# Dilated attention: a maximum pass over 66 rows and value products of 128 columns

## The chip, the cores and the metric

One core of one Trainium2 chip runs the whole program. The metric is the device time of one execution in microseconds (us), as the median of several runs. The engines are TensorE (PE, matrix products, with a queue of its own for loading weights, PEld), VectorE (DVE), ScalarE (ACT), GpSimd (POOL) and SyncE (SP, which issues transfers). The granted TensorE clock is given as a share of 2.4 GHz: 1.00 is that level and 0.50 is 1.2 GHz.

## What is computed

Two transformer blocks over 1024 tokens. The change lies in the second block, in its attention of eight heads of 64 channels: three dilated causal patterns, each with its own softmax, joined by their log sums. That is the same as one softmax in which a pair of tokens counts as often as patterns hold it.

```python
DILATED_PATTERNS = ((128, 1), (512, 4), (2048, 16))

def _dilated_attention(q, k, v):
    ...
    for window, dil in DILATED_PATTERNS:
        ...
        o, lse = _banded_causal_attention(by_stride(q), by_stride(k), by_stride(v), window // dil)
        ...
    wts = jax.nn.softmax(jnp.stack(lses), axis=0)
    o = jnp.sum(wts[..., None] * jnp.stack(outs), axis=0)
    return o.transpose(0, 2, 1, 3)

def second_block(...):
    ...
        o = _dilated_attention(q, k, v)
        o = _rmsnorm(o, attn_norm_gain[l].reshape(ATTN_HEADS, HEAD_DIM)).astype(x.dtype)
        y_attn = o.reshape(B, S, ATTN_WIDTH)
        x = x + jnp.concatenate([y_rwkv, y_attn], axis=-1) @ w_out[l]
```

## The kernel before

Large products are made of pairs of rounded float32 pieces (fp32r, high and low part); in the trace such a product is one matmul record. Products of plain float32 are two records each, one after the other, each with its own weight load.

The attention (`attn`) works head by head, and each head in 12 pieces: a piece is one block of 128 keys (k) against up to 512 queries (half ch of the tokens). For each piece:

- `score` makes the scores by keys in two products: L1811 over 128 rows (the high part of q and its remainder, stacked in `qq`, against the high part of k twice in `kk`) and L1812 over 66 rows (64 rows of the remainder of k in `kl` against the high part of q in `qm`, and two rows in which `kl` is one and `qm` holds minus the maximum of each query, as high and low part).
- `masked` adds the mask on DVE (tile pT, L149), and ACT takes the exponential (L159).
- `gather` multiplies blocks of 128 queries of pT with the values (L1834). The values of a pair of heads lie in `vx` as [128 tokens, 8 blocks, 2 heads, 65]: 64 channels and a one, so that the 65th column of the product is the sum of the weights. Plain float32: 36 products a head, 72 records. The sums stand in bank "a" as [128, 4, 65].

The maximum of a query is found ahead, for a later head, in `attn_max`: 12 pairs of products a head, L1728 over 128 rows and L1729 over 64 rows, after each pair a reduction on DVE (L1730); then a transposition (L1736), two small operations (mh) and two transfers over DRAM that bring the maxima into rows 64 and 65 of `qm`. `attn_heads` makes the operands of a head: four loads, copies of q and k on ACT (L1706, L1709, L1712), two subtractions of about 2.4 us on POOL (qq, kl). `qm` and `kl` have three buffers, taken in turn.

The order on PE, DVE and ACT is written out by hand: score of piece p+1, mask of p, one or two steps of `attn_max` or `attn_heads` of a later head (`ahead`), exponential of p, gather of p-1, a step of transpositions (`attn_values` L1757, `attn_norm` L1789) and, from the second head on, a step of `mix_rwkv` (L1582, the output projection of the other half of the block). POOL and SP, and the group norm of the recurrence that still runs beside the first two heads (L1554, tiles yn, bon, gn, yr), are placed by a scheduler. The maxima of head 0 are found before the loop, beside the end of the recurrence.

Lines below are those of the kernel before; the changed kernel's lie one or two further on.

Of the kernel before, what the change touches and what calls it, by code (L numbers as in the profile page):

```python
# [8 lines left out]
F32 = mybir.dt.float32  # L9
# [3 lines left out]
ALU = mybir.AluOpType  # L13
# [4 lines left out]
P = 128  # L18
# [14 lines left out]
NT = 256            # tokens of a stretch around the recurrence  # L33
NU = T2 // P        # its stretches, of four chunks each
SLOT = 1056
FILL = 12           # piece of the attention from which on the recurrence goes through the output projection
NMM = 3             # accumulator banks of the large products

CH1 = [(0, 352), (352, 696), (696, 1040)]
F0 = 12             # first token that the channel mixer of block 1 sees  # L40
HF = 514            # half of its tokens
# [7 lines left out]
class Build:  # L49
    def __init__(self, ctx, tc, I, out):  # L50
        self.tc, self.nc, self.I, self.out = tc, tc.nc, I, out
        self.const = ctx.enter_context(tc.tile_pool(name="const", bufs=1))
        self.glob = ctx.enter_context(tc.tile_pool(name="glob", bufs=1))
        self.tags = {"XHa": (self.glob, 4), "XHb": (self.glob, 4), "XLa": (self.glob, 4), "XLb": (self.glob, 4), "R": (self.glob, 1), "T": (self.glob, 3)}
        self.wp = ctx.enter_context(tc.tile_pool(name="wp", bufs=2))
        for t in ("wraw", "whi", "wlo"):
            self.tags[t] = (self.wp, 2)
        self.dr = ctx.enter_context(tc.tile_pool(name="dr", bufs=1, space=DRAM))
        self.n, self.sm, self.nsq, self.rdg = 0, None, 2, "T"
        self.turn = {"XH": 1, "XL": 1}      # tags whose slots lie in two sets, taken in turn  # L60

# [6 lines left out]
    def region(self, name, **tags):  # L68
        """a stretch of the program with its own working memory: slots by tag, and small tiles."""
# [9 lines left out]
    def then(self, outer, first, tags, second):  # L79
        """the Y slots through, over them the first region's tags and, from the call of what it yields, the mixer's."""  # L80
# [10 lines left out]
    def psum(self, ctx):  # L91
        """the eight banks of the accumulators: three for the large products, the others by use."""
        self.pp = ctx.enter_context(self.tc.tile_pool(name="ps", bufs=1, space=PSUM))
        self.use, self.nq, self.nmm = {}, 0, 0
        self.big = [f"m{i}" for i in range(NMM)]      # those of the large products
# [14 lines left out]
    def pack(self, sizes, name="pk", tag="S"):  # L110
        """one slot cut into [128, n] pieces."""
# [32 lines left out]
    def store(self, out, in_):  # L144
        """a transfer that waits for data just made: not in the way of the loads."""
# [15 lines left out]
    def split(self, src, shape, name="hl", hi_eng="act", tag=("XH", "XL")):  # L161
        """src (float32) as the exact sum of two float32r tiles."""
# [12 lines left out]
    def weights(self, segs, gain=None):  # L175
        """segs of (source [kt*128 rows, m columns], k offset, column offset) as one [128, kt, m] (hi, lo) pair,
        rows scaled by gain [128, kt]."""
# [15 lines left out]
    def mm3(self, ps, a, b, start, stop, **kw):  # L193
        """ps += a^T b for a, b given as (hi, lo) float32r pairs."""
# [5 lines left out]
    def proj(self, w, rhs, chunks, sink, m0=0, m=P):  # L200
        """sink(ci, a, b, psum[m, b-a]) for each chunk of w^T rhs; w (hi, lo) [128, kt, *]."""
# [9 lines left out]
    def constants(self):  # L211
# [7 lines left out]
        self.triu = self.cst([P, P], name="triu")         # 1 where row <= column  # L219
# [3 lines left out]
        self.sgn = self.cst([P, 1], name="sgn")           # 1 on the upper partitions, -1 on the lower ones  # L223
# [7 lines left out]
    def more_constants(self):  # L231
        nc = self.nc
        self.mpos = self.cst([P, P], name="mpos")         # 0 where row <= column, else huge
# [13 lines left out]
    def params(self, specs):  # L247
        """Vectors of length n*128 as columns: {name: AP [128, n]}."""
# [39 lines left out]
    def add_sums(self, ps, src, start, stop):  # L288
        """ps [128, blocks] += the sums over partitions of src, tokens on the partitions."""
# [8 lines left out]
    def rstd(self, ps, w, n, out=None):  # L298
        """(ps / n + eps)^-0.5 for w tokens, on every partition: an accumulator, or out."""
# [15 lines left out]
    def square_acc(self, acc, src, j, a, b, scale=1.0):  # L315
        """acc[:, a:b] gathers the squares of the tiles j = 0, 1, .."""
# [7 lines left out]
    def square_sum(self, ps, src, start, stop, scale=1.0):  # L324
        """ps += the sums over partitions of the squares of src."""
# [5 lines left out]
    def rstd_chunk(self, out, acc, a, b, n):  # L331
        """out[:, a:b] = (sum over partitions of acc[:, a:b] / n + eps)^-0.5 on every partition."""
# [37 lines left out]
    def spill_x(self):  # L370
        """the residual stream to DRAM while the mixer runs."""
# [24 lines left out]
    def reduce_angle(self, r, x, shape):  # L396
        """r = x mod 2 pi in [-pi, pi]."""
# [6 lines left out]
    def angle_tables(self, cos, sin, rhi, rlo, idx, ng, n, work, sgn):  # L404
        """cos and sin (times a sign per partition) of idx * r for idx [128, n], r = rhi + rlo [128, ng]."""
# [18 lines left out]
    def ssm_params(self):  # L424
# [43 lines left out]
        self.tt(ais, ais, mg, ALU.mult)          # [im; -im] of abar^j  # L468
        nsg = self.cst([P, 1], name="nsg")
        self.ts(nsg, self.sgn, -1.0, ALU.mult)  # L470
        self.ts(ain, ais, nsg[:, 0:1], ALU.mult)         # -im on both halves
        self.ts(ars, ar, self.sgn[:, 0:1], ALU.mult)     # [re; -re]
        self.ars, self.ain = ars, ain
        # input matrices, discretised: z = (abar - 1) / lambda
# [14 lines left out]
        self.ts(zi, zi, nsg[:, 0:1], ALU.mult)   # [-im; im]  # L489
# [15 lines left out]
        # abar^(7-r)  # L505
# [5 lines left out]
        # output matrices  # L511
# [11 lines left out]
        self.c1s, self.dd = (g16(t) for t in self.pack([512, 512], "c1s", "Y"))     # [re; -im]  # L523
        self.dd = self.dd[:16]
        self.ts(self.c1s, self.c1, self.sgn[:, 0:1], ALU.mult)
        # feed-through on the diagonal
# [6 lines left out]
    def ssm_tables(self, j):  # L533
        """lhsT matrices of the eight groups of batch j: chunk input to state, within chunk, state to output."""
# [43 lines left out]
    def ssm_in(self, j):  # L578
        """projection of channels 128 j.. of u, regrouped as [(step, channel), group, chunk]."""
# [54 lines left out]
    def ssm_out(self, j, dy):  # L634
        """gelu of the branch, channels on partitions, tokens in order."""
# [24 lines left out]
    def qko(self):  # L660
        """q and k after convolution and silu, tanh(o / 2), by heads, to DRAM."""
# [15 lines left out]
    def values(self):  # L677
        """v by tokens (with a column of ones) and the input and forget gates by tokens."""
# [36 lines left out]
    def gate_math(self):  # L715
# [11 lines left out]
        # log sigmoid: min(f, 0) - log(1 + exp(-|f|))  # L727
# [19 lines left out]
        # running maximum within each chunk  # L747
# [6 lines left out]
        # running maximum over chunks, on one partition  # L754
# [37 lines left out]
    def conv_qk(self, j, j0, dst):  # L792
        """causal convolution of four taps and silu of tile j of [q, k]."""
# [15 lines left out]
    def mlstm_head(self, h):  # L809
# [57 lines left out]
        # h = num / max(|den|, exp(-m)); then the rms over the head  # L867
# [43 lines left out]
    def merge_a(self, ya):  # L911
        """four times the state space branch, gated."""
# [9 lines left out]
    def merge_b(self, ma, yb):  # L922
        """four times the gated sum of the branches, split."""
# [17 lines left out]
    def rows(self, weights, rhs, ch, acc, sink, scale, apart, between={}):  # L941
        """all output tiles for the token chunks ch, and the inverse rms of what sink returns of them, by chunks;
        apart: the last two tiles chunk by chunk. between[j]: what comes in after tile j."""
# [28 lines left out]
    def mix_out(self, mg, leave):  # L972
        """x += rmsnorm(merged w_out); normed, the operands of the channel mixer."""
# [58 lines left out]
    # The first products go by halves of the channels (the even and the odd tiles of x), of the hidden tiles and of the tokens, seven products of  # L1032
    # halves for eight: with a = w^T = [[a11, a12], [a21, a22]], x = [[x11, x12], [x21, x22]] and
    #   s1 = a21 + a22, s2 = s1 - a11, s3 = a11 - a21, s4 = a12 - s2,
    #   t1 = x12 - x11, t2 = x22 - t1, t3 = x22 - x12, t4 = x21 - t2:
    #   c11 = a11 x11 + a12 x21,               c12 = a11 x11 + s2 t2 + s1 t1 + s4 x22,
    #   c21 = a11 x11 + s2 t2 + s3 t3 + a22 t4, c22 = a11 x11 + s2 t2 + s3 t3 + s1 t1.
    def unit(self, fx, src, c0, dst, fine=False):
        """dst[i] [128, 2 n] = the products for columns c0 + 128 i .. of src, i = 0, 1."""
# [66 lines left out]
    def hidden(self, fx, w_gate, w_up, cw, cb, func):  # L1106
        """func(conv(x w_gate)) * (x w_up), tile by tile to DRAM."""
# [3 lines left out]
        off = 2 * n - T2                # tokens before the first one of the result  # L1111
        z = max(0, 2 - off)             # zeros before those
# [20 lines left out]
    def down(self, hid, w_down, y, last, each=None, after=None, between=None):  # L1133
        """y tiles [128, 1024] = hid w_down, two hidden tiles at a time; each and after by the last ones' chunks."""
# [32 lines left out]
    def ffn1(self, fx):  # L1167
# [8 lines left out]
        def each(j, a, b):  # L1176
            """the sums of squares: while the second half's products run, and after them."""
# [46 lines left out]
    def constants2(self):  # L1224
        nc, g = self.nc, self.nc.gpsimd
        self.blk = self.cst([P, P], name="blk")          # 1 within a head of 64 channels
# [3 lines left out]
        # masks of the products within a chunk: of removal key and key, tokens of the first on the partitions; of removal and  # L1230
        # receptance; of removal and removal key, where twice the removal comes in
# [9 lines left out]
    def lora_weights(self):  # L1241
        """the up-projections of the low rank maps, split: [hi; hi; lo] for the narrow ones."""
# [891 lines left out]
```

## Time and profile before

| | |
|---|---|
| time, median of 3 runs | 3405.7 us (3387.16, 3406.9, 3405.7) |
| profiled execution, span from first to last instruction | 3405.0 us |
| PE busy | 3186.8 us (94%) |
| DVE, ACT, POOL busy | 2026.2, 1145.8, 1336.8 us |
| mean granted TensorE clock over the span | 0.900 |
| attention loop, from head 0 to the end of head 7 | 2253.0 to 2581.8 us of the span |

The span of the profiled execution is its own time as far as the profile tells; it stands 0.7 us under the median. Busy time of PE is made of records whose ends are modelled, so the distance from the start of one record to the start of the next says more of a product's cost than its length. A row of the timeline gives the start, the length of what is merged in it (x8 is eight records), the engine, the line and the tiles.

### The profile page before, as it was taken

The page shows a single profiled execution, that of the slowest core. Times are in us where ns is not written, and L with a number is a line of the kernel's source. Part 1 is how long each engine was busy: PE and PEld are TensorE (multiplying, and loading weights), DVE is VectorE, ACT ScalarE, POOL GpSimd, SP SyncE. Part 2 cuts the span into 40 slices and gives each one's busy share as a digit, 9 for nine tenths or more (in the row PEclk, how much of TensorE's full clock was granted, in tenths as well). Part 3 has the DMA queues.
Part 4 walks back from the last instruction along what each step waited for, and adds up shares of the span by engine and source line. Part 5 has one row for each costly group of instructions (what it writes and reads, how often), then busy time and mean ns, then how long its engine had stood idle before and what let it go on. Part 6 is the DMA issues. An engine that isn't in the chain of part 4 may idle for free.

```text
span 3405.0 us, 52731 instructions
## 1 busy us (share of the span) xinstructions
PE 3186.8 (94%) x20636; PEld 2789.2 (82%) x20636; DVE 2026.2 (60%) x3567; ACT 1145.8 (34%) x2178; POOL 1336.8 (39%) x1303
## 2 busy tenths in 40 slices
PE   4989999989799999999999898999998799999998
PEld 3989999879799999877777787867767688887777
DVE  4565563674676666466866544464444866665666
ACT  2334323344343344312432333322323433334211
POOL 5666210133554443323531645421101655554431
PEclk7999999989799999999799888855758799999999
DMA  4434422334222222421334544322215222224321
GB/s 134 98 88 109 133 94 60 101 112 134 69 75 75 76 80 92 145 92 52 112 117 151 143 110 116 102 81 68 81 54 181 73 87 75 82 89 157 130 75 56
DMA packets 322534, 336.82 MB, mean 99 GB/s; under 512 B 60081, under 2 KB 270734, under 8 KB 322286
## 3 DMA queue, kind: packets, MB, share of 16 engines
q1 hardware_dynamic: 289646, 310.38, 29.9%
q10 hardware_dynamic: 32640, 23.08, 2.1%
q8 instruction: 162, 2.65, 0.3%
q14 instruction: 86, 0.70, 0.1%
HBM read 232.66 MB, written 96.40 MB: 97 GB/s over the span
## 4 chain that ended last, share of the span: by engine, by line
PE 72%; DVE 9%; issue 4%; POOL 3%; DMA 3%; ACT 3%; SPq 1%; ACTq 0%; DVEq 0%; POOLq 0%
PE pm L196 13%; PE pm L197 13%; PE pm L198 13%; PE px L197 5%; PE px L196 5%; PE px L198 5%; PE pa L1834 3%; PE pm L1729 2%; DVE dn L149 2%; PE pc L1582 1%; PE pc L1502 1%; PE pm L1728 1%; DVE t L149 1%; PE px L292 1%; POOL fs L149 1%
## 5 line engine op out<-in xcount | busy, mean ns | idle before, releaser
L196 PE MATMUL pm<-xh,whi 128*128 128x512 f32 (+5 forms) x1344 | 454.0, 338 | 15.2 <-DVE th L149 9.4
L198 PE MATMUL pm<-xh,wlo 128*128 128x512 f32 (+5 forms) x1344 | 453.0, 337 | 0.9 <-DVE wlo L149 0.9
L197 PE MATMUL pm<-xl,whi 128*128 128x512 f32 (+5 forms) x1344 | 453.2, 337 | 0.0
L149 DVE TENSOR_TENSOR y<-y,pm 128x512 f32<-128x512 f32 (+1 forms) x336 | 218.1, 660 | 159.5 <-PE pm L198 159.1
L196 PEld LDWEIGHTS pm<-xh,whi 128*128 128x128 f32 (+1 forms) x1344 | 263.2, 196 | 38.2 <-DVE th L149 9.8
L196 PE MATMUL pm<-dn,dn 128*128 128x512 f32 (+1 forms) x736 | 285.8, 389 | 6.7 <-DVE y L149 6.3
L197 PE MATMUL pm<-dn,dn 128*128 128x512 f32 (+1 forms) x736 | 282.9, 384 | 0.7 <-POOL dn L149 0.7
L198 PE MATMUL pm<-dn,dn 128*128 128x512 f32 (+1 forms) x736 | 282.6, 384 | 0.0
L198 PEld LDWEIGHTS pm<-xh,wlo 128*128 128x128 f32 (+1 forms) x1344 | 262.6, 195 | 22.2 <-DVE wlo L149 1.3
L197 PEld LDWEIGHTS pm<-xl,whi 128*128 128x128 f32 (+1 forms) x1344 | 263.2, 196 | 20.7 <-issue 0.9
L149 POOL TENSOR_TENSOR dn<-hid,dn 128x1024 fp32r<-128x1024 f32 x44 | 131.8, 3014 | 250.6 <-ACT dn L1141 250.6
L197 PE MATMUL px<-t,sh 128*128 128x258 f32 (+2 forms) x684 | 218.5, 320 | 3.2 <-DVE t L149 3.2
L196 PE MATMUL px<-t,sh 128*128 128x258 f32 (+2 forms) x684 | 216.4, 317 | 1.5 <-DVE up L149 1.5
L198 PE MATMUL px<-t,sl 128*128 128x258 f32 (+2 forms) x684 | 216.2, 316 | 0.0
L149 DVE TENSOR_TENSOR wlo<-wraw,whi 128x1024 fp32r<-128x1024 f32 (+2 forms) x114 | 152.5, 1340 | 82.5 <-ACT whi L170 79.9
L196 PEld LDWEIGHTS pm<-dn,dn 128*128 128x128 f32 x736 | 138.2, 188 | 44.3 <-DVE y L149 14.4
L170 ACT CAST whi<-wraw 128x1024 fp32r<-128x1024 f32 (+2 forms) x114 | 103.2, 906 | 186.4 <-PE pm L197 147.6
L198 PEld LDWEIGHTS pm<-dn,dn 128*128 128x128 f32 x736 | 138.3, 188 | 29.8
L197 PEld LDWEIGHTS pm<-dn,dn 128*128 128x128 f32 x736 | 138.4, 188 | 29.5 <-POOL dn L149 1.2
L149 POOL TENSOR_TENSOR wraw<-wraw,par 128x1024 f32<-128x1024 f32 (+1 forms) x36 | 72.4, 2010 | 191.9 <-DMA wraw<-in_w_in_dram 183.5
L170 ACT CAST dn<-wd 128x1024 fp32r<-128x1024 f32 x44 | 46.1, 1047 | 291.1 <-PE pm L197 290.6
L197 PEld LDWEIGHTS px<-t,sh 128*128 128x128 f32 x684 | 130.5, 191 | 14.4 <-DVE t L149 5.3
(601 smaller groups left out, 9016.0 us busy)
## 6 DMA issues: line engine op xcount, KB each, us to landing
wraw<-in_w_in_dram SPq DMA_DIRECT2D x61, 512.0 KB
dhid<-up SPq DMA_DIRECT2D x44, 512.0 KB
wd<-in_w_ffn_down_dram SPq DMA_DIRECT2D x44, 512.0 KB
hid<-dhid SPq DMA_DIRECT2D x44, 512.0 KB
wra<-in_w_ffn_up_dram SPq DMA_DIRECT2D x33, 512.0 KB
wrb<-in_w_ffn_up_dram SPq DMA_DIRECT2D x33, 512.0 KB
dg<-th SPq DMA_DIRECT2D x16, 514.0 KB
wraw<-in_w_out_dram SPq DMA_DIRECT2D x16, 512.0 KB
```

Of the source, the lines that this page charges most:

```text
L149: (eng or self.nc.vector).tensor_tensor(out=o, in0=a, in1=b, op=op)
L170: self.nc.scalar.copy(hi, src)
L196: nc.tensor.matmul(ps, a[0], b[0], start=start, stop=False, **kw)
L197: nc.tensor.matmul(ps, a[0], b[1], start=False, stop=False, **kw)
L198: nc.tensor.matmul(ps, a[1], b[0], start=False, stop=stop, **kw)
L292: self.nc.tensor.matmul(ps[:bw, i:i + 1], src[:, i * bw:i * bw + bw], self.ones[:, 0:1], start=start and i == 0, stop=stop and i == n - 1)
L1502: nc.tensor.matmul(ps[:, h], maps[c][:, h], S[:, h], start=True, stop=True)
L1582: nc.tensor.matmul(ps, w[:, k], (yh, yl, yh)[q][:, a:b], start=i == 0, stop=i == 11)
L1728: nc.tensor.matmul(ps, qq[:, qs], kk[:, a:bb], start=True, stop=False)
L1729: nc.tensor.matmul(ps, qm[:64, qs], kl[:64, a:bb], start=False, stop=True)
L1834: nc.tensor.matmul(self.po[:, i - 4 * ch], pT[:, i * P - a:i * P - a + P], self.vx[j % 2][:, k, e], start=k == 0 and i == 4 * ch, stop=k = ...
```

## The change

The second product of the maximum pass takes 66 rows of both operands instead of 64. So that the two added rows give nothing, rows 64 and 65 of `qm` are set to zero on POOL when the operands of the head are made; the maxima are written over them later, as before. The value product takes 128 neighbouring columns of the 130 that a pair of heads has in `vx`, from column 0 for the first head and from column 2 for the second, into a bank of [128, 4, 128]; the 64 channels and the sum are picked from columns 0 to 64, or 63 to 127, and the other columns are not used. The rest of the full difference takes out comments and moves no instruction.

```diff
@@ attn_heads
         nc.scalar.copy(qm[:64], raws[0][:64])
+        pool.memset(qm[64:66].bitcast(F32), 0.0)
         yield
@@ attn_max
                 nc.tensor.matmul(ps, qq[:, qs], kk[:, a:bb], start=True, stop=False)
-                nc.tensor.matmul(ps, qm[:64, qs], kl[:64, a:bb], start=False, stop=True)
+                nc.tensor.matmul(ps, qm[:66, qs], kl[:66, a:bb], start=False, stop=True)
@@ gather
             if k == 0:
-                self.po = self.bank([P, 4, 65], "a")
+                self.po = self.bank([P, 4, P], "a")
...
-                nc.tensor.matmul(self.po[:, i - 4 * ch], pT[:, i * P - a:i * P - a + P], self.vx[j % 2][:, k, e],
+                nc.tensor.matmul(self.po[:, i - 4 * ch], pT[:, i * P - a:i * P - a + P],
+                                 self.vx[j % 2][:, k].rearrange("p e v -> p (e v)")[:, 2 * e:2 * e + P],
                                  start=k == 0 and i == 4 * ch, stop=k == last)
...
-                    nc.scalar.copy(on[:, bs, e], po[:, :, :64])
-                    nc.scalar.copy(st[:, 0, bs, e:e + 1], po[:, :, 64:])
+                    nc.scalar.copy(on[:, bs, e], po[:, :, 63 * e:63 * e + 64])
+                    nc.scalar.copy(st[:, 0, bs, e:e + 1], po[:, :, 64 + 63 * e:65 + 63 * e])
```

On POOL, around the operands of heads 4 and 5 (qq and kl are the subtractions of `attn_heads`), the kernel before has:

```order
L149 TENSOR_TENSOR on_22757<-on_22757,af_23227 128x1024
L149 TENSOR_TENSOR qq_23346<-raw_23348,qq_23346 64x1024
L149 TENSOR_TENSOR kl_22256<-raw_23349,kk_23347 64x1024
L149 TENSOR_TENSOR qq_23597<-raw_23599,qq_23597 64x1024
L149 TENSOR_TENSOR kl_22257<-raw_23600,kk_23598 64x1024
```

And the changed kernel has:

```order
L149 TENSOR_TENSOR on_22759<-on_22759,af_23231 128x1024
L149 TENSOR_TENSOR qq_23350<-raw_23352,qq_23350 64x1024
L1713 MEMSET qm_22260 2x1024
L149 TENSOR_TENSOR kl_22256<-raw_23353,kk_23351 64x1024
L149 TENSOR_TENSOR qq_23602<-raw_23604,qq_23602 64x1024
L1713 MEMSET qm_22258 2x1024
L149 TENSOR_TENSOR kl_22257<-raw_23605,kk_23603 64x1024
```

The zeroing stands between the two subtractions of a head, and it is that of the head after (qm_22260 is the third buffer, that of head 5).

On PE, in the second half of head 0, the kernel before has this order (L1554 is a transposition of the group norm):

```order
L1834 MATMUL pa_22756<-vx_22261,pT_22768 128x65
L1811 MATMUL pm_3196_22810<-qq_22631,kk_22632 128x512
L1812 MATMUL pm_3196_22810<-qm_22258,kl_22255 128x512
L1554 MATMUL pq_3115_22480<-ident_66,yn_22453 128x128 x2
L1728 MATMUL pm_3197_22814<-kk_22649,qq_22648 128x448
L1729 MATMUL pm_3197_22814<-kl_22256,qm_22259 128x448
```

And the changed kernel has:

```order
L1835 MATMUL pa_22758<-vx_22261,pT_22770 128x128
L1812 MATMUL pm_3196_22812<-qq_22631,kk_22632 128x512
L1813 MATMUL pm_3196_22812<-qm_22258,kl_22255 128x512
L1729 MATMUL pm_3197_22816<-kk_22650,qq_22649 128x448
L1730 MATMUL pm_3197_22816<-kl_22256,qm_22259 128x448
L1835 MATMUL pa_22820<-vx_22261,pT_22798 128x128 x4
```

The products of the attention keep their order; some transpositions of the group norm in heads 0 and 1, and what hangs on them on DVE, ACT, POOL and SP, come some pieces later.

## Rows read from the trace of the kernel before

**Rows 1.** Page, granted TensorE clock in 40 slices of 85 us, in tenths.

```profile
PEclk7999999989799999999799888855758799999999
```

**Rows 2.** Busy time by stretch: us, PE, PEld, DVE, ACT, POOL, clock, DMA share, GB/s.

```profile
2253.00:2292.50 39.50, 39.50 (x129) 29.72 (x128) 30.68 (x96) 13.40 (x27) 12.36 (x10) 0.50 0.24 73
2292.50:2339.90 47.40, 43.66 (x161) 31.60 (x159) 27.32 (x78) 15.62 (x33) 12.07 (x10) 0.64 0.35 99
2339.90:2562.50 222.60, 216.39 (x767) 159.25 (x767) 93.94 (x251) 61.55 (x121) 24.67 (x11) 0.62 0.22 63
2388.50:2419.30 30.80, 28.70 (x153) 21.36 (x153) 17.59 (x41) 12.03 (x24) 4.74 (x2) 0.99 0.44 127
2562.50:2581.80 19.30, 19.01 (x122) 16.31 (x121) 8.82 (x16) 8.67 (x21) 0.00 (x0) 1.00 0.39 117
```

**Rows 3.** The same view, stretches between changes of the clock.

```profile
2340.00:2384.30 44.30, 44.30 (x134) 32.80 (x133) 17.81 (x53) 10.18 (x20) 4.25 (x2) 0.50 0.15 44
2384.40:2418.40 34.00, 31.55 (x172) 23.40 (x171) 18.27 (x43) 14.51 (x29) 7.13 (x3) 1.00 0.43 123
```

**Rows 4.** Timeline of PE, maximum pass of head 0, clock 0.50.

```profile
2241.32 0.79 PE L1729 MATMUL pm<-kl,qm 64*128 64x512 f32 x1
2242.04 0.79 PE L1728 MATMUL pm<-kk,qq 128*128 128x512 f32 x1
2242.76 0.79 PE L1729 MATMUL pm<-kl,qm 64*128 64x512 f32 x1
```

**Rows 5.** Timeline of PE, scores by keys, clock 0.50.

```profile
2309.15 0.63 PE L1811 MATMUL pc<-qq,kk 128*128 128x512 f32 x1
2309.58 0.63 PE L1812 MATMUL pc<-qm,kl 66*128 66x512 f32 x1
2310.01 0.63 PE L1554 MATMUL pq<-ident,yn 128*128 128x128 f32 x2
```

**Rows 6.** Timeline of PE, scores, maximum pass and values, clock 1.00.

```profile
2403.82 0.39 PE L1812 MATMUL pc<-qm,kl 66*128 66x512 f32 x1
2404.06 0.39 PE L1728 MATMUL pm<-kk,qq 128*128 128x512 f32 x1
2404.38 0.49 PE L1729 MATMUL pm<-kl,qm 64*128 64x512 f32 x1
2404.80 0.50 PE L1728 MATMUL pm<-kk,qq 128*128 128x512 f32 x1
2405.23 0.50 PE L1729 MATMUL pm<-kl,qm 64*128 64x512 f32 x1
2405.66 1.11 PE L1834 MATMUL pa<-vx,pT 128*128 128x65 f32 x8
2406.60 0.61 PE L1757 MATMUL pq<-ident,vT 128*128 128x128 f32 x4
```

**Rows 7.** Timeline of PE, eight value records at clock 0.50.

```profile
2281.85 1.81 PE L1834 MATMUL pa<-vx,pT 128*128 128x65 f32 x8
2283.41 0.67 PE L1811 MATMUL pc<-qq,kk 128*128 128x384 f32 x1
```

**Rows 8.** Timeline of PE, plain float32 products of the first block, clock 1.00.

```profile
190.85 0.61 PE L627 MATMUL px<-z,ct 128*128 128x130 f32 x4
191.30 0.39 PE L626 MATMUL px<-u,tp 128*128 128x130 f32 x2
...
192.94 0.35 PE L563 MATMUL px<-ct,bb 128*16 128x112 f32 x2
193.13 0.20 PE L562 MATMUL px<-c1s,bb 128*16 128x16 f32 x2
```

**Rows 9.** Timeline of PE, four transpositions before the clock's rise at 2384.4.

```profile
2381.78 1.06 PE L1789 MATMUL pq<-ident,on 128*128 128x128 f32 x4
```

**Rows 10.** Timeline of all engines, the change from head 3 to head 4.

```profile
2415.51 2.35 POOL L149 TENSOR_TENSOR kl<-raw,kk 64x1024 fp32r<-64x1024 f32 x1
...
2416.14 2.28 DVE L149 TENSOR_TENSOR wo<-wo,wo 128x512 fp32r<-128x512 f32 x1 [3.74 <-ACT wo L170]
...
2418.67 0.69 PE L1811 MATMUL pc<-qq,kk 128*128 128x384 f32 x1 [1.84 <-DVE pT L149]
```

**Rows 11.** Groups of POOL by line and shape: xcount | busy us, mean ns | idle.

```profile
L1513 POOL MEMSET xt<- 128x1024 f32 x1 | 0.9, 944 | 0.0
```

## The prediction

> **What bounds the kernel now.** I first read the page's row of the granted clock: it is near full nearly everywhere, and low in the slices from 2213 to 2570 us, the attention [rows 1]. Then the busy time by stretch, one for head 0, one for head 1, one for heads 2 to 6, and head 7 [rows 2]. PE is busy for 39.5 of 39.5 us, 43.7 of 47.4, and 216.4 of 222.6, at a mean clock of 0.50, 0.64 and 0.62; DVE has 30.7 and 27.3 us in heads 0 and 1, but 93.9 of 222.6 later, and ACT less. So PE sets the time from head 1 on, and it does so at half its clock for most of it. What full clock is worth, head 3 shows: it alone ran through at 0.99 and took 30.8 us (the fourth line of [rows 2]), where the other four of heads 2 to 6 took (222.6 - 30.8) / 4 = 48.0 each.
>
> Next the timeline of PE at both levels. In the maximum pass the products of 64 rows stand apart: at 0.50 a product of 512 columns takes 0.72 us from start to start, be it L1729 to L1728 or back [rows 4], while the scores, with 66 rows and the same columns, take 0.43 [rows 5]. At 1.00 it is 0.42 to 0.43 around L1729 and 0.24 from L1812 (66 rows) to L1728 [rows 6]. So a change between 128 and 64 rows costs 0.29 us at 0.50 and 0.19 at 1.00, in each direction, and one between 128 and 66 costs nothing: the weight load is hidden in one case and stands bare in the other.
>
> Last the changes of the clock. It stays at 0.50 from 2340.0 to 2384.3, then at 1.00 to 2418.4 [rows 3]; there are five rises inside the loop, and each comes within 5 us after a run of four transpositions of 128 columns (one such run is in [rows 9]), in a stretch without a maximum pair. All four falls inside the loop come where PE has stood still at the change of a head (1.84 us before L1811 in the one of [rows 10]). What ran during the low stretches is the same for all: pairs with bare weight loads, and value records of 65 columns.
>
> **Part 1, 66 rows.** 12 pairs a head, 24 products, each with one change of rows that no longer costs anything: 24 x 0.29 = 7.0 us a head at 0.50, 24 x 0.19 = 4.6 us at 1.00. For head 0, whose pass runs ahead of the loop at 0.50 [rows 4], it is up to 20 x 0.29 = 6, but what follows there is a chain of transfers and the group norm; I take 3, bounds 0 and 6. Two more rows stream at no cost: 66 rows in rows 5 run at 0.43 for 512 columns, as 128 do.
>
> **Part 2, 128 columns.** Eight value records take 1.56 us at 0.50 (2281.85 to 2283.41) [rows 7] and 0.94 at 1.00 [rows 6]: about 0.195 and 0.117 each. If the columns set this pace, 128 would double it. They don't: plain float32 products of 130 columns go at 0.45 / 4 = 0.112 us each at 1.00 [rows 8], as 65 do. What 65 columns take by themselves follows from L563, where the weights are only 16 columns: 112 columns take 0.19 / 2 = 0.095 us [rows 8], so 65 take 0.055 and 128 take 0.109, just under the pace. Inside a run the added 0.054 is covered by the weight load; at the first and the last record of a run it may show: 2 x 0.054 = 0.11 us for each of 96 runs, 1.3 us a head at 1.00. I take that in full; the lower bound is nothing. The Trainium skill ("TensorE: Matmul & The Clock Gate", back-to-back issue gap) speaks against this edit: it gives about 60 cycles for up to 64 columns and 134 for 128. By it 576 records would cost 576 x 74 cycles, an estimate of 18 us at 2.4 GHz; the rows of 130 columns decide otherwise. The copies of the sums on ACT keep their number of elements.
>
> **Part 3, the clock.** With both edits PE has no bare loads in the pairs and nearly twice the streaming time in the value runs, so every stretch of the loop looks like the stretches that the rises followed. I expect the clock at 1.00 for most of the loop. Then heads 2 to 6 are like head 3: 30.8 - 4.6 + 1.3 = 27.5 us. PE idles for 2.1 of the 30.8, DVE has 17.6 of work and ACT 12.0 [rows 2]; with a shorter PE some waits for mask and exponential will come out, so I take 28.5 (an estimate; bounds 27.5 and 31). 5 x 28.5 = 142.5 against 222.6: -80 (-85 to -68). Heads 0 and 1 have 58.0 us of DVE work in 86.9 us [rows 2]; PE at full clock would be done sooner, so DVE becomes their bound, and with some idle time I take 64 (59 to 72): -23 (-28 to -15). Head 7 ran at 1.00 and has no maximum pass: +1.
>
> **What comes up.** At the change of a head PE stood still because ACT and DVE were late with copies and with a subtraction that took 2.28 us beside one on POOL [rows 10]. That stays and is in head 3's 30.8. But the clock may fall there, as it did. If each of six changes brings 7 us at half clock, that is 6 x 3.5 = 21 us; if none does, nothing. I take +8. The zeroing on POOL takes at most 0.94 us, the price of 128 x 1024 [rows 11], and stands before the kl subtraction of a head; it waits for the last score of the head that had the buffer. Behind it are kl, and behind that the first L1729 of the next pass, on PE. That score is issued about one piece before, so for five heads I take +2 (0 to 5).
>
> **The sum.** -80 - 23 + 1 - 3 + 8 + 2 = -95 us on a span of 3405.0, which stands 0.7 under the median of 3405.7: **3310 us**. With the bounds at their best it is -85 - 28 - 6 + 0 = -119, 3286; at their worst -68 - 15 + 1 + 21 + 5 = -56, 3349. What follows the loop is unchanged and only starts earlier.
>
> **Rivals.**
> *The clock stays as it was.* Then only bare loads go: 168 products in the loop, three quarters at 0.50 by the mean of 0.62, give 168 x (0.75 x 0.29 + 0.25 x 0.19) = 45, and 3 ahead of it; the ends of value runs cost twice 0.11 at 0.50, some 15: 3405.7 - 33 = 3373. For it: stretches of dense fp32r products at 0.50 without a rise (the 44 us of rows 3 are all busy). Against: those held pairs throughout. 8%.
> *The 66 rows change nothing.* The bare load would belong to the pass and not to the 64 rows. Then heads 2 to 6 take 30.8 + 1.3 each, -62, heads 0 and 1 perhaps -12, with +8 and +1: 3341. Against: rows 5 and 6 show the same operands at 66 rows without it. The Trainium skill (same page, LDWEIGHTS) would have it so, since a load's time goes by columns and rows don't matter; the trace agrees on its length, and shows that hiding is another matter. 4%.
> *Slower: wide records cost in proportion.* Place: L1834 in the loop, 576 records. If 128 columns run at 128/65 of 0.195 and 0.117, each adds 0.19 at 0.50 and 0.114 at 1.00. With the clock low it is +109 against -48: 3405.7 + 61 = 3467; with the clock up, +65 against -95: 3376. It decides from a pace of about 0.2 us a record at 1.00. Against: 130 columns at 0.112 [rows 8]. 3% for the slow end.
> *The clock rises but falls at each change of head for as long as now.* Half of what the clock gives is lost: about 3340, inside the range. 10%.
>
> **How the numbers follow.** The forecast has 75%. The range takes in its bounds and the second and fourth rival, and leaves out the first and third: 3283 to 3352. This kernel can tell about 1%, 34 us, from no change. Faster by more than that are the forecast, the second, the fourth and half of the first: 0.92; within it the rest of the first and the mild end of the third: 0.05; slower 0.03.
>
> **What would show it.** Granted clock at or near 1.00 in the loop, where it was 0.50 to 0.64; L1729 (then L1730) to L1728 at 0.24 us for 512 columns; eight value records in 0.9 to 1.05 us; heads 2 to 6 at 27.5 to 31 us; DVE busy for over 85% of heads 0 and 1. I am wrong if the value records go at 0.2 us or more at 1.00, if the clock is at 0.50 for more than a third of the loop, or if a head takes over 33 us at 1.00 because PE waits for the exponential.

## The result, and the profile after

The changed kernel takes 3295.5 us (median of 4 runs, 3292.1 to 3298.3), the kernel before 3406.1 on the same chip (3387.2 to 3406.9): a ratio of 0.971, 95% interval 0.967 to 0.975. The forecast was 3310, with a range of 3283 to 3352. The profiled execution spans 3295.9 us against 3405.0, so 109.1 us less.

The page of the changed kernel, its span and its row of the granted clock:

```profile
span 3295.9 us, 52738 instructions
...
PEclk7999999989779999999989978787998799999999
```

The slices of the attention, 0.5 to 0.8 before [rows 1], now read 7 or more. Where the time went is told by the stretches of [rows 2], which begin with the first exponential of a head. The busy time by stretch of the changed kernel, for head 0, head 1, heads 2 to 6, and head 7:

```profile
2246.60:2276.30 29.70, 24.57 (x132) 20.14 (x131) 26.53 (x85) 12.57 (x25) 12.06 (x10) 0.84 0.27 82
2276.30:2314.70 38.40, 28.86 (x157) 24.91 (x158) 29.47 (x90) 15.38 (x32) 14.07 (x12) 0.83 0.43 124
2314.70:2453.70 139.00, 130.02 (x768) 111.06 (x768) 92.32 (x254) 61.53 (x123) 28.36 (x16) 0.95 0.35 103
2453.60:2473.00 19.40, 19.06 (x121) 16.37 (x121) 8.81 (x16) 8.72 (x22) 0.00 (x0) 1.00 0.37 123
```

Heads 2 to 6 take 139.0 us where they took 222.6 (-83.6), at a mean clock of 0.95 instead of 0.62. Heads 0 and 1 take 68.1 instead of 86.9 (-18.8), head 7 the same. The loop as a whole goes from 328.6 us (2253.2 to 2581.8) to 226.4, which is -102.2; it starts 6.6 earlier, and what follows it takes 822.9 against 823.2. That is the whole difference.

How the clock behaves now is seen in three stretches between its changes. The first and the last are at full clock (the first reads 0.97, since it takes in the last 3.4 us of the low stretch before it), and between them lies the longest low stretch that heads 2 to 6 still have:

```profile
2306.60:2364.60 58.00, 54.82 (x336) 47.26 (x334) 39.35 (x105) 29.70 (x57) 17.08 (x11) 0.97 0.45 130
2368.00:2374.80 6.80, 6.56 (x23) 5.99 (x24) 2.99 (x11) 1.91 (x4) 0.19 (x1) 0.50 0.47 114
2375.00:2398.60 23.60, 21.35 (x130) 17.47 (x130) 16.57 (x45) 10.52 (x20) 7.51 (x4) 1.00 0.28 82
```

A low stretch lasted 44.3 us in [rows 3]; the six that begin inside the loop now last 3.4 to 6.8.

The timeline of PE at full clock, the counterpart of [rows 6]: two maximum pairs and the value records behind them.

```profile
2343.31 0.34 PE L1729 MATMUL pm<-kk,qq 128*128 128x384 f32 x1
2343.49 0.34 PE L1730 MATMUL pm<-kl,qm 66*128 66x384 f32 x1
2343.66 0.40 PE L1729 MATMUL pm<-kk,qq 128*128 128x512 f32 x1
2343.89 0.40 PE L1730 MATMUL pm<-kl,qm 66*128 66x512 f32 x1
2344.13 1.05 PE L1835 MATMUL pa<-vx,pT 128*128 128x128 f32 x8
2344.94 0.71 PE L1582 MATMUL pc<-yr,wo 128*128 128x512 f32 x2
```

From start to start a maximum product of 512 columns takes 0.23 to 0.24 us (0.42 to 0.43 before), and eight value records take 0.81 (0.94 in [rows 6], behind a product of 64 rows and with a transposition next).

The zeroing stands where the prediction placed it, ahead of the subtraction for kl, with PE behind both. The timeline of all engines at the change from head 3 to head 4:

```profile
2364.53 0.95 POOL L1713 MEMSET qm<- 2x1024 f32 x1
...
2365.55 2.64 POOL L149 TENSOR_TENSOR kl<-raw,kk 64x1024 fp32r<-64x1024 f32 x1
...
2368.24 0.58 PE L1730 MATMUL pm<-kl,qm 66*128 66x256 f32 x1 [1.27 <-POOL kl L149]
```

The zeroing ends, the subtraction for kl starts behind it, and PE stands 1.27 us before the first L1730 of the pass. The low stretch from 2368.0 begins right there. Over the loop the waits of PE and of its weight queue for kl read as follows (us in total, times, the longest):

```profile
PEld pm L1730 <- POOL kl L149: 3.2, 2, 1.7
PE pm L1730 <- POOL kl L149: 2.7, 2, 1.4
```

These are the same two places, seen from both queues: the change from head 0 to head 1, and the one above. PE stands for 2.7 us in all. The 5.9 us and the four waits that some of the expectations below name are the sum of both rows, so they count each place twice.

Head 1 is the one stretch in which PE stands for long. The timeline of SP, DVE and PE there:

```profile
2301.80 0.35 SPq L142 DMA_DIRECT2D xo<-dx  x1
...
2305.08 0.69 DVE L149 TENSOR_TENSOR xo<-xo,pc 128x512 f32<-128x512 f32 x1 [0.98 <-DMA xo<-dx]
...
2305.82 1.22 PE L1582 MATMUL pc<-yr,wo 128*128 128x512 f32 x2 [4.09 <-DVE xo L149]
```

The second tile of the output projection needs the accumulator of the first. That one is free once DVE has added it to xo, whose load was issued only at 2301.80, so PE stands for 4.09 us.

### The profile page after: what moved, and what is told of

It reads as the page before. It is cut to its first block, busy times and chain, and to the rows that moved or that the text cites. A ratio compares the mean times of both kernels' runs of the same rounds, so it can differ in the third digit from the quotient of the medians.

```text
span 3295.9 us, 52738 instructions
## 1 busy us (share of the span) xinstructions
PE 3061.8 (93%) x20636; PEld 2723.7 (83%) x20636; DVE 2024.9 (61%) x3567; ACT 1145.1 (35%) x2178; POOL 1347.9 (41%) x1311
## 4 chain that ended last, share of the span: by engine, by line
PE 69%; DVE 11%; issue 4%; POOL 4%; DMA 3%; ACT 3%; SPq 1%; ACTq 0%; DVEq 0%; POOLq 0%
PE pm L196 14%; PE pm L197 14%; PE pm L198 14%; PE px L197 5%; PE px L196 5%; PE px L198 5%; DVE dn L149 2%; PE pc L1502 1%; DVE t L149 1%; PE px L292 1%; PE pa L1835 1%; POOL fs L149 1%; POOL Z L149 1%; DVE zs L614 1%; PE pm L1474 1%
```

## The experiments

The experiments come in three groups, each timed on one chip with the kernel before beside it: e1 to e4, e5 to e8, and the last four rows (medians of the kernel before 3394.3, 3398.0 and 3396.3 us). Each was run four times (e8b five). The kernel before itself differs by up to 12 us from group to group (3394.3 to 3406.1), so a few us between groups tell nothing. The loop's length and granted clock are of the profiled execution of each.

| run | median us (range) | ratio, 95% interval | loop us | clock in it |
|---|---|---|---|---|
| changed kernel | 3295.5 (3292.1 to 3298.3) | 0.971, 0.967 to 0.975 | 226.4 | 0.92 |
| e1_rows_only | 3309.9 (3309.4 to 3320.0) | 0.975, 0.971 to 0.979 | 244.8 | 0.80 |
| e2_columns_only | 3335.0 (3332.6 to 3340.5) | 0.982, 0.978 to 0.986 | 250.7 | 0.92 |
| e3_zero_on_dve | 3295.4 (3286.6 to 3299.7) | 0.970, 0.965 to 0.976 | 220.1 | 0.95 |
| e4_zero_once | 3295.5 (3293.1 to 3297.4) | 0.970, 0.966 to 0.974 | 228.5 | 0.92 |
| e5_both_64 | 3352.7 (3334.0 to 3358.1) | 0.985, 0.979 to 0.992 | 264.8 | 0.80 |
| e6_96_columns | 3301.1 (3299.6 to 3302.7) | 0.971, 0.965 to 0.978 | 228.6 | 0.91 |
| e7_dve_fill16 | 3290.3 (3283.3 to 3293.9) | 0.968, 0.962 to 0.973 | 213.3 | 0.94 |
| e8_dve_fill20 | 3289.0 (3282.8 to 3294.0) | 0.967, 0.962 to 0.973 | 211.8 | 0.96 |
| a1_changed_again | 3293.3 (3289.8 to 3302.2) | 0.969, 0.966 to 0.972 | 225.2 | 0.93 |
| e3b_dve_again | 3294.5 (3290.6 to 3304.9) | 0.970, 0.967 to 0.972 | 223.0 | 0.93 |
| e8b_dve_fill20_again | 3291.7 (3289.2 to 3295.7) | 0.968, 0.966 to 0.971 | 211.3 | 0.96 |
| e9_fill20 | 3289.6 (3283.6 to 3291.7) | 0.967, 0.965 to 0.970 | 213.2 | 0.95 |

**Each part alone.** e1 is the kernel before with 66 rows and the zeroing, 65 columns:

```diff
+        pool.memset(qm[64:66].bitcast(F32), 0.0)
-                nc.tensor.matmul(ps, qm[:64, qs], kl[:64, a:bb], start=False, stop=True)
+                nc.tensor.matmul(ps, qm[:66, qs], kl[:66, a:bb], start=False, stop=True)
```

> The maximum pass with 66 rows (and the zeroing), the value products with 65 columns as before. My theory: the bare weight loads of the pass are gone whatever the clock does (0.24 us from product to product of 512 columns at clock 1.00, 0.43 at 0.50), worth about 45 us of the 110; the clock rises in part only, since the value runs are as thin as before: 3310 to 3345 us, with a granted clock in the loop between that of before (0.62 in heads 2 to 6) and that of the change (0.95). Rival (the rows do everything, the columns nothing): 3296 us and a clock of 0.95. Rival (the columns do everything): 3406 us.

e2 is the kernel before with 128 columns, 64 rows and no zeroing:

```diff
-                self.po = self.bank([P, 4, 65], "a")
+                self.po = self.bank([P, 4, P], "a")
...
+                                 self.vx[j % 2][:, k].rearrange("p e v -> p (e v)")[:, 2 * e:2 * e + P],
```

> The value products with 128 columns, the maximum pass with 64 rows and no zeroing. My theory: the bare loads stay (0.42 us per product of 512 columns at clock 1.00), the clock is up for most of the loop: 3335 to 3355 us, heads 2 to 6 at 31 to 36 us. Eight value records take no longer than with 65 columns. Rival (the columns do nothing for the clock): 3406 us or a little more. Rival (the columns do everything): 3296 us.

Both came out at the lower edge of what was expected (3309.9 for 3310 to 3345, 3335.0 for 3335 to 3355). In the loop the rows alone are worth 328.6 - 244.8 = 83.8 us, the columns alone 77.9, both 102.2: the two gains overlap by 59.5, because each raises the clock of the loop by itself, from 0.63 to 0.80 and to 0.92. What each does is read from the rows. The timeline of PE in e2 at full clock:

```profile
2353.11 0.40 PE L1728 MATMUL pm<-kk,qq 128*128 128x512 f32 x1
2353.44 0.49 PE L1729 MATMUL pm<-kl,qm 64*128 64x512 f32 x1
2353.86 0.49 PE L1728 MATMUL pm<-kk,qq 128*128 128x512 f32 x1
2354.28 0.49 PE L1729 MATMUL pm<-kl,qm 64*128 64x512 f32 x1
2354.71 1.16 PE L1834 MATMUL pa<-vx,pT 128*128 128x128 f32 x8
2355.62 0.70 PE L1582 MATMUL pc<-yr,wo 128*128 128x512 f32 x2
```

The bare loads are all there, 0.42 us between starts as in [rows 6], and the eight value records behind a product of 64 rows take 0.91. In e1, at full clock as well, the loads are gone and the eight records of 65 columns behind a product of 66 rows take 0.81:

```profile
2339.91 0.39 PE L1729 MATMUL pm<-kk,qq 128*128 128x512 f32 x1
2340.14 0.39 PE L1730 MATMUL pm<-kl,qm 66*128 66x512 f32 x1
2340.38 0.50 PE L1729 MATMUL pm<-kk,qq 128*128 128x512 f32 x1
2340.71 0.40 PE L1730 MATMUL pm<-kl,qm 66*128 66x512 f32 x1
2340.95 1.00 PE L1835 MATMUL pa<-vx,pT 128*128 128x65 f32 x8
2341.76 0.70 PE L1582 MATMUL pc<-yr,wo 128*128 128x512 f32 x2
```

The products follow each other at 0.23 to 0.24 us; the one step of 0.33 lies behind a weight load that waited 0.27 us for DVE. The 0.81 us are those of the changed kernel with 128 columns. So at full clock the wide records cost nothing and gain nothing; the step from 0.91 to 0.81 belongs to the rows, by the load at the front of the run. Whole heads say the same: head 3 of the kernel before takes 30.8 us and head 3 of e2 30.9, both at full clock; head 6 of e1 takes 26.9 and of the changed kernel 27.0, both at 0.95.

What the columns do is hold the clock up. e1 has stretches at half clock of 10 to 27 us each in heads 0 to 4; two of them, the busy time by stretch:

```profile
2271.90:2299.10 27.20, 25.66 (x98) 23.22 (x98) 22.68 (x66) 11.08 (x23) 12.14 (x10) 0.50 0.36 99
2319.70:2336.60 16.90, 16.73 (x58) 15.32 (x59) 9.47 (x31) 4.21 (x9) 0.41 (x1) 0.50 0.29 83
```

In the second PE is busy for 16.73 of 16.90 us, without one bare load, and the clock doesn't rise. In e2 the clock stays up for 64.8 us at a stretch although the bare loads are there:

```profile
2333.20:2398.00 64.80, 60.55 (x326) 44.80 (x325) 41.10 (x104) 26.86 (x54) 15.33 (x9) 1.00 0.40 114
```

**A dose between 65 and 128 columns.** e6 has both edits with 96 columns:

```diff
-                nc.tensor.matmul(self.po[:, i - 4 * ch], pT[:, i * P - a:i * P - a + P],
-                                 self.vx[j % 2][:, k].rearrange("p e v -> p (e v)")[:, 2 * e:2 * e + P],
+                nc.tensor.matmul(self.po[:, i - 4 * ch, :96], pT[:, i * P - a:i * P - a + P],
+                                 self.vx[j % 2][:, k].rearrange("p e v -> p (e v)")[:, 34 * e:34 * e + 96],
```

> Both edits, but value products of 96 columns. If the gain of the wide value products (3295.5 with 128, 3309.9 with 65, both with 66 rows) follows the columns, this gives 3300 to 3306 and stretches at 0.50 in the loop of 6 to 15 us. If it comes from the step between a value record and the next product, and that step is short for any width well over 65 (31 ns against 83 ns at 1.00), this gives 3293 to 3299 and the step reads 30 to 40 ns. If only 128 columns shorten it, 3306 to 3313 and 80 ns.

The time, 3301.1, and the low stretches, 6.8 to 10.2 us long, lie in the first theory's ranges. The time alone doesn't decide: the three were timed in different groups, and beside the kernel before on its own chip e6 has the ratio of the changed kernel, 0.971. The mean granted clock over the whole span does better, as it was read in every run: 0.919 to 0.923 with 65 columns, 0.926 to 0.930 with 96, 0.929 to 0.932 with 128. Heads 2 to 6, as a stretch of e1, of e6 and of e2, in this order in three views (the third, with 128 columns but 64 rows, is for the account further down):

```profile
2320.40:2473.30 152.90, 143.60 (x770) 124.76 (x768) 92.59 (x251) 61.36 (x121) 27.61 (x14) 0.85 0.30 90
```

```profile
2313.70:2453.90 140.20, 131.01 (x769) 112.17 (x767) 92.14 (x254) 61.44 (x123) 28.39 (x16) 0.94 0.35 102
```

```profile
2337.50:2493.10 155.60, 148.33 (x769) 109.77 (x767) 93.63 (x253) 61.76 (x123) 25.42 (x12) 0.97 0.31 92
```

With 65, 96 and 128 columns and 66 rows these heads take 152.9, 140.2 and 139.0 us at 0.85, 0.94 and 0.95 (135.9 at 0.97 in the second profile of the changed kernel): most of the effect is there at 96. The step from the last value record to the next product is 57 ns at 96 columns, between 83 and 31 and not the 30 to 40 that the second theory asks for. It can't be the reason for a gain either, since eight records with the step behind them take 0.81 us at each of the three widths.

**64 rows in both products.** e5 asks whether it is the 64 rows that make a load stand bare, or the change of rows:

```diff
-                nc.tensor.matmul(ps, qq[:, qs], kk[:, a:bb], start=True, stop=False)
-                nc.tensor.matmul(ps, qm[:66, qs], kl[:66, a:bb], start=False, stop=True)
+                nc.tensor.matmul(ps, qq[:64, qs], kk[:64, a:bb], start=True, stop=False)
+                nc.tensor.matmul(ps, qm[:64, qs], kl[:64, a:bb], start=False, stop=True)
```

> Left out: the low part of q against the high part of k in the maximum pass (its first product takes 64 rows, not 128), so the maxima are a little less exact; everything else as in the changed kernel. Both products of the pass now have 64 rows. If a weight load stands bare because its neighbour has another count of rows, two records inside the pass follow each other at the hidden pace (about 0.24 us for 512 columns at 1.00, 0.43 us at 0.50), only the steps to and from other products are bare, and the time is 3292 to 3308. If a load of 64 rows stands bare beside any neighbour, every record of the pass takes 0.42 to 0.43 us at 1.00 and 0.72 us at 0.50, as in the kernel with 128 columns alone, and the time is 3325 to 3345.

The timeline of PE in e5, two pairs at full clock with a score ahead of them and value records behind:

```profile
2348.56 0.40 PE L1813 MATMUL pc<-qm,kl 66*128 66x512 f32 x1
2348.89 0.49 PE L1729 MATMUL pm<-kk,qq 64*128 64x512 f32 x1
2349.23 0.39 PE L1730 MATMUL pm<-kl,qm 64*128 64x512 f32 x1
2349.46 0.39 PE L1729 MATMUL pm<-kk,qq 64*128 64x512 f32 x1
2349.68 0.39 PE L1730 MATMUL pm<-kl,qm 64*128 64x512 f32 x1
2350.01 1.16 PE L1835 MATMUL pa<-vx,pT 128*128 128x128 f32 x8
2350.92 0.71 PE L1582 MATMUL pc<-yr,wo 128*128 128x512 f32 x2
```

From start to start: 0.33, 0.34, 0.23, 0.22, 0.33. Inside the run of 64 rows the load is hidden (0.22 to 0.23 us); at its front, twice, and at its end it stands bare (0.33 to 0.34). So the change of rows makes the load stand bare, and the first theory is right on the spacing. The Trainium skill ("TensorEngine Tiling (Array Packing)", Key Properties) says that switching the tiling mode drains the engine; its list of modes (Available Configurations) has 64 rows as one of its own. The trace agrees as far as the bare steps lie at the edges of a run, with 0.10 us each, though at the front there are two of them. Both theories missed the time, 3352.7, which is longer than either's range. The loop is at half clock for long again, though no product in it has fewer columns than in the changed kernel. Heads 2 to 6 of e5:

```profile
2330.70:2503.30 172.60, 164.09 (x770) 125.64 (x768) 94.51 (x254) 61.80 (x123) 29.02 (x16) 0.81 0.28 81
```

They take 33.6 us more than in the changed kernel, at 0.81 instead of 0.95. The bare steps alone don't explain that clock: e2 has 0.42 us from product to product in its pass and still reads 0.97 in these heads, at 155.6 us. In the products, what e5 has and e2 has not is a first product of 64 rows instead of 128; why the clock is lower with it the runs don't show.

**The zeroing.** e3 moves it to VectorE, e4 does it once ahead of the loop (and leaves out the transfer that puts the maxima into the two rows, so that the scores are not reduced by them):

```diff
-        pool.memset(qm[64:66].bitcast(F32), 0.0)
+        nc.vector.memset(qm[64:66].bitcast(F32), 0.0)
```

```diff
+        for qm in self.qm:
+            pool.memset(qm[64:66].bitcast(F32), 0.0)
...
-        pool.memset(qm[64:66].bitcast(F32), 0.0)
...
-            self.dma(out=qm[64:66].bitcast(F32), in_=self.dmx[h].rearrange("r i t -> r (i t)"))
```

> Both edits, the zeroing of two rows moved from POOL to DVE, in the order written by hand. My theory: four waits of L1730 for the subtraction kl on POOL (5.9 us in all, the longest 1.5) come from the zeroing of 0.95 us ahead of it; without it they shrink to under 2 us and head 4 no longer loses its clock at its start: 3288 to 3294 us. Rival (DVE has no room for eight more operations at the change of a head): 3296 to 3302 us, and the waits of ACT for the mask grow.

> Both edits, two rows set to zero once ahead of the heads, and the transfer of the maxima into these rows left out, so that nothing overwrites them: the scores are not reduced by their maximum. My theory: as without any zeroing, 3286 to 3292 us; the transfer itself was not waited for. Rival (the transfer of the maxima holds up the scores of the next head): 3280 us or less.

> Both edits, the zeroing on VectorE, as before. If the 5.9 us that the max products wait for POOL in the changed kernel are worth their length, 3287 to 3291 beside 3295; if what they cost comes back in head 1, within 2 us of the changed kernel.

> The changed kernel itself, so that the three runs beside it are compared on one chip: 3292 to 3298.

The wait is gone from L1730 in e3, and heads 2 to 6 take 132.7 us at 0.99, in e3 as in e4. Their stretch in e3:

```profile
2311.50:2444.20 132.70, 125.07 (x769) 106.91 (x767) 95.32 (x257) 61.42 (x122) 25.44 (x12) 0.99 0.37 108
```

That is 6.3 us less than in the changed kernel. The second profiles of both kernels, a1 and then e3b, are closer to each other:

```profile
2317.40:2453.30 135.90, 126.82 (x768) 108.30 (x767) 91.91 (x253) 61.44 (x123) 28.40 (x16) 0.97 0.36 105
2328.60:2462.80 134.20, 126.47 (x767) 108.22 (x767) 95.51 (x257) 61.45 (x122) 25.46 (x12) 0.97 0.36 106
```

Here the difference is 1.7 us, near the one wait for kl in these heads (1.3 us, in a1 as in the first profile). That wait stood ahead of a fall of the clock in the first profile and not in a1. The rest of the 6.3 us goes with low stretches that differ between executions of one kernel: 13.6 us of them in heads 2 to 6 of the first profile, 6.8 in a1, 3.4 in e3, 6.8 in e3b.

The medians show no gain: 3295.4 and 3295.5 beside 3295.5, and on one chip 3294.5 beside 3293.3. So the theories of e3 and e4 (3288 to 3294, 3286 to 3292) both missed, and so did their rivals; e3b came out as its second branch has it, within 2 us of the changed kernel. In e4 head 1 takes 49.1 us instead of 38.4, with transpositions of the group norm that come one by one, 3.6 to 4.8 us from start to start; in e3 it takes 40.9. What the zeroing on POOL costs in the whole kernel is less than these runs tell (the runs of e3b alone lie 14 us apart).

**Head 1, and a faster kernel.** e7 and e8 are e3 with the output projection from piece 16 or 20 of the loop on, e9 is the changed kernel with 20:

```diff
-FILL = 12
+FILL = 20
```

> Both edits, the zeroing on VectorE, and the recurrence's output projection joins the loop from piece 16 on instead of 12. If the stalls of head 1 (2.5 us and 4.4 us before the projection's products, and the stretch at half clock behind them) come from the projection starting before the group norm is through, they go and the time is 3284 to 3291. If the group norm is late whatever the start, or the steps that leave the loop run bare behind it, the time is 3293 to 3303.

> As the run before it, from piece 20 on. By the first theory it gains no more than with 16 (3282 to 3291, since the wait is over by then); by the second each four pieces of delay leave about four steps of the projection (12 records of 512 columns, some 4 us) for after the loop, and the time is 3297 to 3307.

> Zeroing on VectorE and the projection from piece 20 on, as before: 3286 to 3292, 4 to 8 us below the changed kernel on the same chip, if the gain seen before is real; within 2 us of it if it was noise.

> The changed kernel (zeroing on POOL) with the projection from piece 20 on. If the later start alone gives the gain, as e8b within 2 us; if the place of the zeroing gives it, as the changed kernel; if each gives its own part, between the two, 3290 to 3294.

The loop gets shorter by 12 to 14 us. On one chip, the loop of a1, of e8b and of e9, in three views:

```profile
2247.50:2472.70 225.20, 201.39 (x1171) 171.34 (x1171) 156.66 (x440) 98.03 (x201) 54.52 (x37) 0.93 0.36 106
```

```profile
2254.30:2465.60 211.30, 191.90 (x1156) 164.36 (x1155) 153.14 (x443) 96.40 (x199) 48.52 (x31) 0.96 0.38 107
```

```profile
2251.90:2465.10 213.20, 192.53 (x1155) 165.04 (x1155) 151.20 (x437) 96.06 (x199) 54.09 (x37) 0.95 0.38 106
```

Head 1 goes from 39.8 us in a1 to 31.8 and 30.6. Of the 12 to 14 us, some 3 come back behind the loop (3289.7 - 2465.6 = 824.1 and 3288.5 - 2465.1 = 823.4 against 3293.2 - 2472.7 = 820.5), where the products that left it run, though the first profile of the changed kernel has 822.9 there as well; and these two loops begin 4 to 7 us later. The times are 3291.7 and 3289.6 beside 3293.3, with intervals that overlap. The lowest medians of all runs are those with the later projection (3289.0 to 3291.7), on one chip 1.6 and 3.7 us below the changed kernel; that it gains is likely but not settled. e7 and e8 came out in the first theory's ranges, and the second theory's loss did not come. The repeat was weaker: e8b's 1.6 us fall under "within 2 us of it if it was noise", and e9, 2.1 us below e8b, lies just outside all of its branches. Heads 2 to 6 of e9, with the zeroing on POOL, take 132.0 us, as do those of e8 with it on DVE.

## Why the prediction was right, step by step

**What bounds the kernel, and the mechanism: right.** PE at half clock set the time, the clock rose with both edits, and the bare loads went. Full clock can now be separated from the rows: heads 2 to 6 with 64 rows and a clock of 0.97 take 155.6 us (e2), with 66 rows and 0.99 they take 132.7 (e3). So of 222.6, taken in this order, the clock is worth 67, the rows at full clock 23, and short falls and one wait for kl take back 6.3 of it in the changed kernel: 139.0 (3.2 and 135.9 in a1).

**Part 1, 66 rows: right.** 4.6 us a head at 1.00 was forecast; 30.9 to 26.3 is what head 3 shows between e2 and e3. For the start of the loop 3 us were taken with bounds 0 and 6. The 6.6 measured can't settle it: e3 and e3b are the same kernel and begin at 2243.5 and 2259.3.

**Part 2, 128 columns: mis-sized.** The +1.3 us a head is nothing (0.81 us for eight records at 65 as at 128 columns). The lower bound held; the 0.05 us at either end of a run shows only in the runs of eight that stand before a transposition, with 0.89 us instead of 0.84. The forecast of 0.9 to 1.05 us for eight records was too long, since the rows of before that it leaned on had a bare load at the front of the run [rows 6]. The Trainium skill ("TensorE: Matmul & The Clock Gate", back-to-back issue gap) has, in its table for products by themselves, 128 columns cost over twice what up to 64 do. For these plain float32 records, each behind a weight load of its own, the trace shows no such step between 65 and 128 columns, with 0.81 us for eight at either.

**Part 3, the clock: right in kind, 2 us a head too careful.** 28.5 us for a head at full clock; five heads with one fall of 3.4 us take 132.7 / 5 = 26.5 (e3). Of the 2.0 between them 1.3 is the columns, and 0.7 the waits for mask and exponential, which were taken at 1.0 and hardly came out. So heads 2 to 6 came to 139.0 where 142.5 + 8 + 2 = 152.5 was forecast; this is the step that was off, by 13.5 us of the 14 between a forecast of -95 and the span's -109. That nothing else shows in the sum is luck: heads 0 and 1 were 4.1 us longer than forecast and the loop began 3.6 earlier, and the two cancel. Single heads took 24.8 to 31.9 us, 27.8 on average.

**Heads 0 and 1: 68.1 for 64.** DVE is busy for 26.53 of 29.70 us in head 0, which is 89% and the bound that was named. In head 1 it is 29.47 of 38.40, or 77%, not the 85% forecast: there the order of the projection and the load of xo make PE and DVE wait for each other, as the 4.09 us above show. With the later projection the two heads take 27.1 + 31.8 = 58.9 in e8b, but DVE is then busy for only 24.9 + 26.6 = 51.5 of them, as part of its work has moved to later heads; that this meets the lower end of 59, which rested on 58.0 of DVE work, is chance. The prediction had looked at the busy time of DVE and not at the order in which it works.

**What comes up: +10 forecast, 6.3 and 3.2 measured.** This is heads 2 to 6 of the two profiles of the changed kernel against the 132.7 of e3. The falls last 3.4 to 6.8 us each (up to 10.2 in a1), as the 7 us that were taken, but come at four changes of a head and not at six. PE waits 2.7 us for kl behind the zeroing in the whole loop (3.0 in a1), where +2 (0 to 5) was forecast: right. The zeroing itself doesn't wait for the buffer: POOL is idle for 0.1 us ahead of its six zeroings together. That a wait for kl can bring a fall of the clock was not in the forecast; both did in the first profile, one of two in a1.

**The rivals.** The clock stays as it was: refuted by 0.92 in the loop (its price had a slip: the ends of the value runs come to 96 x (0.75 x 0.22 + 0.25 x 0.11) = 18 us and not some 15, which makes it 3376). The 66 rows change nothing: refuted by e1, and by the steps of 0.23 us. Wide records cost in proportion: refuted, 112 ns from record to record with 65, 96 and 128 columns. The clock falls as long as now at each change of a head: refuted, 6.8 us at most and 10.2 in a1, where it was 34 to 44.

**What stays open.** That the loop with products of 65 columns stays at half clock with PE busy and no bare load, and that e5 loses as much as it does, the traces show; why, they don't.

## What to carry to other kernels

Look at the rows of neighbouring products: a product of 64 rows among products of 66 or 128 puts its weight load and the next one in the open (0.19 us each at full clock here, 0.29 at half), and two idle rows of zeros close the gap. If PE is busy and its granted clock is 0.50, it is worth trying more columns in the narrow products: here they cost nothing in the pace of a record (112 ns) and took 78 us out of the loop by themselves. Two edits that raise the same clock don't add up (83.8 and 77.9 us each alone, 102.2 together), and before a busy engine is called the bound of a stretch, read the order in which it works. A few us between two profiles can be the clock of one execution: profile both kernels again before giving them to an edit, as the 6.3 us of the zeroing became 1.7.

## What the runs showed of the hardware

- Wider products went with a higher clock: with 65, 96 and 128 columns in the value products the granted clock of heads 2 to 6 was 0.85, 0.94 and 0.95 (0.97 in a1), with the same products otherwise.
- A run of 64-row products hides its loads inside and not at its edges: 0.22 to 0.23 us against 0.33 to 0.34 in e5.
- Zeroing 2 partitions of 1024 columns on POOL takes as long as 128 of them: 0.95 us here, 0.944 in [rows 11].
